# Up projection of an encoder layer: 21 instead of 14 of 64 row pairs by seven products, the transposes of a group together, and an order for VectorE where the stage begins

## The chip, the core and the metric

The kernel runs on one core of a Trainium2 chip. The metric is the device time of one execution in microseconds (us); the time of a kernel is the median over its runs. PE is TensorE (matrix products), DVE is VectorE, ACT is ScalarE, POOL is GpSimd, SP is the engine whose queue issues most of the loads. L649 is line 649 of the kernel.

## What is computed

One layer of an encoder for 256 tokens of 2048 channels: a projection, two kinds of attention, gates, an output projection, and an MLP with squared ReLU. The change lies in the up projection, the first half of the MLP (line 2 below), and a little of it in what stands just ahead.

```python
x = x + rms_norm(y, norm_mix_post)            # y: output projection, 256 x 2048
h = rms_norm(x, norm_mlp_pre)
u = square(relu(h @ w_up))                    # w_up: 2048 x 8192, float32, 64 MB
x = x + rms_norm(u @ w_down, norm_mlp_post)
```

## The kernel before, in words

Products are made in float32 accuracy from halves: a number is split into a high half (a cast to fp32r on ACT, tiles `...h`) and the rest (a subtraction on DVE, tiles `...l`), and each product is three matmuls: high x high, high x low, low x high. The activations are the stationary side (`h2T`, transposed by PE through an identity matrix), the weights the moving side, 512 columns at a time.

**Groups and pairs.** The up projection runs over 8 groups of 1024 columns (`for g in range(DFF // 1024)`); names `u_3h` and so on leave out the group. In a group, `wide_group` runs over 8 pairs of 128-row slices of `w_up` (pair i is 256 rows x 1024 columns, 1 MB, one load by SP, L606). The result of a group stands in PSUM banks 1, 2, 3 and 7 (2 token halves x 2 column halves).

**Eight products.** A pair with eight products (flag 0) casts all of `raw` to `hi` on ACT (L609, 128x2048), takes the rest on DVE (L610), and makes 4 bank pieces x 2 slices x 3 = 24 matmuls.

**Seven products.** A pair with seven (flag 1) is Winograd's form of Strassen's scheme for a 2 x 2 block product: `pair_weights` casts three of the four blocks (L613, 128x1536) and takes their rest (L617), makes four sums of blocks on DVE (L614, L615, L616, tiles `t`), casts these in two pieces (L626, `eh`) and takes their rest (L627, `el`). `Products.seven` then makes 7 x 3 = 21 matmuls: products 2, 1, 0 from the blocks, and 4, 6, 5, 3 from the sums, in banks 0 to 6. The stationary side needs sums too (`h2s`), made once, in group 0, by `sums_of`. At the last pair with seven, `combine` brings banks 0, 4, 5 and 6 together on ACT and DVE (L676 to L680), and each piece then has its plain bank added (`u_piece`, L1022).

**Buffers.** `raw`, `hi` and `lo` have three buffers each (pool `wp`), so a pair's load waits until an earlier pair's `raw` is read for the last time, and its cast until PE has made the last matmul on an earlier pair's `hi` and `lo`. The tiles `eh` and `el` have five buffers (pool `mid`). The sums `t` and most other tiles come from 27 pages of 4 KB in each partition. PSUM has four banks for 1, 2, 3 and 7, and four that banks 0, 4, 5, 6 share with all transposes.

**What comes between.** While a group runs, the previous group's result is turned and split: `u_sets` transposes 512 columns (8 small matmuls `uT`, L1009), squares them on ACT (L1012), makes sums (`sm`, L952 to L955) for every other set, splits them (`ah` on ACT, `al` on DVE, L967, L968) and writes them to DRAM (POOL's queue, L971). There are two sets to a group, one asked for at pair n = 1 and one at n = 2.

**Order.** The kernel is written tile by tile, and a scheduler with a clock of its own sets the order on each engine: the next instruction of an engine is the first in program order that it takes to be ready then. On the chip each engine keeps that order and waits where an operand is late. Matmuls into one PSUM bank keep program order. `tc.issue_after(x)` holds an instruction back behind x in that order.

**Where the stage begins.** The output projection's last group (`agroup`, L230 to L232) makes the rows of token half t = 0, then t = 1. As soon as half 0 is done, its post norm runs on DVE and POOL (`ry_m`, L86; `ry`, L89), the residual is added (L869), and `between` puts the first transposes (L876) among the last matmuls; ACT and DVE split these into `h2T` (L885, L886). Group 0 has eight products throughout; of its first three pairs t = 0 is made first, then the first residual part of t = 1 (`turn`), then t = 1. `first_up(n)` puts the other parts at n = 2 to 4.

Of the kernel before, what the change touches and what calls it, by code (L numbers as in the profile page):

```python
# [11 lines left out]
F32 = mybir.dt.float32  # L12
F32R = mybir.dt.float32r
AF = mybir.ActivationFunctionType
ALU = mybir.AluOpType
# [8 lines left out]
EPS = 1e-6  # L24
# [14 lines left out]
def encoder_layer(ctx: ExitStack, tc: tile.TileContext, a, out):  # L39
    nc = tc.nc  # L40
# [41 lines left out]
    def inv_rms(ss, n, name, r=None):  # L82

        w = ss.shape[1]
        ms_ = small(w, f"{name}_m")
        nc.vector.tensor_scalar(ms_, ss, 1.0 / n, EPS, op0=ALU.mult, op1=ALU.add)  # L86
        if r is None:
            r = small(w, f"{name}_r")
        nc.gpsimd.tensor_tensor(r, ms_, expo[:, :w], op=ALU.pow)  # L89
        return r  # L90


    last_load = [None]

    def load(src, k0, nk, c0, cw, name):

# [502 lines left out]
    def wtile(tag, name):  # L599
        return wp.tile([P, 4, 512], F32R, tag=tag, name=name)  # L600

    def pair_weights(view, name, seven, low=None):


        raw = wp.tile([P, 4, 512], F32, tag="raw", name=f"{name}r")
        last_load[0] = nc.sync.dma_start(raw.rearrange("p (h b) c -> p h (b c)", h=2), view).ins  # L606
        h1, l1 = wtile("hi", f"{name}h"), wtile("lo", f"{name}l")
        if not seven:
            nc.scalar.copy(h1, raw)  # L609
            nc.vector.tensor_sub(l1, raw, h1.bitcast(F32))  # L610
            return h1, l1
        t = [page([P, 2, 512], F32, f"{name}t{i}") for i in range(2)]
        nc.scalar.copy(h1[:, 1:4], raw[:, 1:4])  # L613
        nc.vector.tensor_add(t[0], raw[:, 1:3], raw[:, 0:1].to_broadcast([P, 2, 512]))  # L614
        nc.vector.tensor_add(t[1][:, 0], t[0][:, 0], raw[:, 2])  # L615
        nc.vector.tensor_add(t[1][:, 1], t[1][:, 0], raw[:, 3])  # L616
        nc.vector.tensor_sub(l1[:, 1:4], raw[:, 1:4], h1[:, 1:4].bitcast(F32))  # L617
        h2, l2 = [], []
        for i in range(2):
            for part, n in ((h2, "eh"), (l2, "el")):  # L620
                shape, n = [P, 2, 512], f"{name}{n}{i}"
                if low and part is l2:
                    part.append(low(shape, F32R, n))
                else:
                    part.append(mid.tile(shape, F32R, tag="e", name=n))
            nc.scalar.copy(h2[i], t[i])  # L626
            nc.vector.tensor_sub(l2[i], t[i], h2[i].bitcast(F32))  # L627
        return h1, l1, h2, l2
# [3 lines left out]
    class Products:  # L632
# [22 lines left out]
        def seven(self, stat, w, last):  # L655


            r, t = w[:2], list(zip(*w[2:]))
            self.add(0, stat(0), r, 1, last)
            self.add(2, stat(6), r, 2)  # L660
            self.add(1, stat(1), r, 3)
            self.add(4, stat(3), t[0], 0, last)
            self.add(6, stat(4), t[0], 1, last)
            self.add(5, stat(5), t[1], 0, last)
            self.add(3, stat(2), t[1], 1)
# [16 lines left out]
    def wide_group(name, kinds, view, stat7, stat8, mm_banks, z, piece, each=None, turn=None):  # L682

        any7 = any(s for _, s in kinds)
        pr = Products(name, mm_banks)
        for n, (i, seven) in enumerate(kinds):
            if each:
                each(n)  # L690
            w = pair_weights(view(i), f"{name}_{i}", seven)
# [58 lines left out]
    ALL8 = [(i, 0) for i in range(8)]  # L750
# [22 lines left out]
    for h in range(2):  # L773
        gate = []
        for br, gc in (("a", GA), ("b", GB)):
# [89 lines left out]
    def residual_parts(t, c, after=None):  # L865
        cs = slice((c % 2) * 512, (c % 2 + 1) * 512)
        xt = x2[t * 2 + c // 2][:, cs]
        with tc.issue_after(after) if after else nullcontext():
            nc.vector.scalar_tensor_tensor(  # L869
                xt, yw[t * 2 + c // 2][:, cs], ry[:, t : t + 1], xt, op0=ALU.mult, op1=ALU.add  # L870
            )
        for h in range(2):
            pt = bank(f"h2T_t{t}{c}{h}")
            for i in range(2):
                kk = h * 2 + i
                last = nc.tensor.transpose(  # L876
                    pt[:, i * P : (i + 1) * P], xt[:, kk * P : (kk + 1) * P], ident
                )
            for i in range(2):
                k = c * 4 + h * 2 + i  # L880
                d = hT2[k // 2][:, k % 2]
                src = pt[:, i * P : (i + 1) * P]
                hi = d[:, t * P : (t + 1) * P]
                g = g_mlp[:, k : k + 1]
                act = nc.scalar.activation(hi, src, AF.Copy, scale=g)  # L885
                vec = nc.vector.scalar_tensor_tensor(  # L886
                    d[:, T + t * P : T + (t + 1) * P],
                    src,
                    g,
                    hi.bitcast(F32),  # L890
                    op0=ALU.mult,
                    op1=ALU.subtract,
                )
        return last.ins, act.ins, vec.ins

    def between(i):
        return residual_parts(0, i - 5)[0] if i in (5, 6) else None

    def mlp_squares(t):
        for c in range(4):  # L900
# [25 lines left out]
    def first_up(n):  # L926
        for t, c in {2: [(1, 1), (0, 2)], 3: [(1, 2), (0, 3)], 4: [(1, 3)]}.get(n, ()):
            residual_parts(t, c)
        if n == 5:
            for t in range(2):  # L930
                mlp_squares(t)
                mlp_scale(t)
# [68 lines left out]
    def u_sets(cg, z):  # L1001

        u = page([P, 4, T], F32, f"u{cg}")
        for b in range(2):
            pt = bank(f"uT{cg}{b}")
            for j in range(2):
                for t in range(2):
                    c = (b * 2 + j) * P
                    nc.tensor.transpose(  # L1009
                        pt[:, j * T + t * P : j * T + (t + 1) * P], z[t][:, cg % 2, c : c + P], ident  # L1010
                    )
            nc.scalar.activation(  # L1012
                u[:, b * 2 : b * 2 + 2], pt.rearrange("p (j q) -> p j q", j=2), AF.Square
            )
        got = act_sets(cg, u)
        if NG - 4 <= cg < NG - 2:
            sets[0, cg] = got
# [4 lines left out]
            nc.vector.tensor_add(zt, zt, ps)  # L1022
        nc.scalar.activation(zt, zt if summed else ps, AF.Relu, scale=r2[:, t : t + 1])

    UPS = [(0, 0), (1, 0), (2, 0), (3, 1), (4, 0), (5, 1), (6, 0), (7, 0)]
    uz = None
    for g in range(DFF // 1024):
        z = [page([P, 2, 512], F32, f"u{g}{t}") for t in range(2)]

        def up_each(n, g=g, uz=uz):  # L1030
            if not g:
                first_up(n)
                if n == 7:
                    for i in (3, 5):
                        f = page([P, 2, T], F32, f"h2f{i}")
                        for k in range(2):
                            d = hT2[i][:, k].bitcast(F32)
                            nc.vector.tensor_add(f[:, k], d[:, :T], d[:, T:])
                        h2sum[i] = sums_of(f[:, 0], f[:, 1], f"h2s{i}")
            elif n in (1, 2):  # L1040
                u_sets(g * 2 - 3 + n, uz)

        wide_group(
            f"u{g}",
            UPS if g else ALL8,
            lambda i, c=g * 1024: a["w_up"][i * T : (i + 1) * T, c : c + 1024].rearrange(
                "(k p) c -> p k c", p=P
            ),
            h2stat7,
            h2stat8,  # L1050
            (1, 2, 3, 7),
            z,
            partial(u_piece, z=z),
            each=up_each,
            turn=None if g else partial(residual_parts, 1, 0),
        )
        uz = z

# [140 lines left out]
```

## Time and profile before

| | |
|---|---|
| median of 3 runs | 1370.4 us (1367.77 to 1371.29) |
| profiled execution | 1367.94 us, of which the span is 1366.2 us |
| granted PE clock | 0.997 of full speed |
| PE busy | 1340.7 us, 98% of the span |
| DVE busy | 1034.7 us, 76% |
| ACT busy | 717.8 us, 53% |
| up projection, groups 1 to 7 | about 44 us each (752.28 to 796.29 is one) |

Instructions are told with start, duration, engine, line, and the idle time of their engine just before them in brackets, with what ended it. A row with x3 holds three of a kind. Starts are us from the span's start.

### The profile page before, as it was taken

The page shows a single profiled execution, that of the slowest core. Times are in us where ns is not written, and L with a number is a line of the kernel's source. Part 1 is how long each engine was busy: PE and PEld are TensorE (multiplying, and loading weights), DVE is VectorE, ACT ScalarE, POOL GpSimd, SP SyncE. Part 2 cuts the span into 40 slices and gives each one's busy share as a digit, 9 for nine tenths or more (in the row PEclk, how much of TensorE's full clock was granted, in tenths as well). Part 3 has the DMA queues.
Part 4 walks back from the last instruction along what each step waited for, and adds up shares of the span by engine and source line. Part 5 has one row for each costly group of instructions (what it writes and reads, how often), then busy time and mean ns, then how long its engine had stood idle before and what let it go on. Part 6 is the DMA issues. An engine that isn't in the chain of part 4 may idle for free.

```text
span 1366.2 us, 16268 instructions
## 1 busy us (share of the span) xinstructions
PE 1340.7 (98%) x6347; PEld 1119.4 (82%) x6347; DVE 1034.7 (76%) x1181; ACT 717.8 (53%) x843; POOL 33.9 (2%) x67
## 2 busy tenths in 40 slices
PE   7999999999999999999999999999999999999996
PEld 6888888888888888888788888888887788888885
DVE  6878866667857886654768887888788888798886
ACT  7455455555644464344465655666555555454542
POOL 0000000000000000000000000000000000000000
PEclk9999999999999999999999999999999999999998
DMA  8675645564556655676367766786697999698891
GB/s 306 201 227 168 202 161 175 166 206 154 185 185 213 218 185 185 204 264 205 134 207 260 259 244 243 258 287 231 249 336 282 386 355 373 239 385 346 340 352 74
DMA packets 115245, 329.57 MB, mean 241 GB/s; under 512 B 17120, under 2 KB 18400, under 8 KB 115168
## 3 DMA queue, kind: packets, MB, share of 16 engines
q1 hardware_dynamic: 96784, 264.03, 56.1%
q10 hardware_dynamic: 12240, 40.91, 7.7%
q0 software_dynamic: 6144, 23.60, 4.3%
q8 instruction: 50, 0.82, 0.2%
q14 instruction: 27, 0.22, 0.0%
HBM read 302.81 MB, written 27.51 MB: 242 GB/s over the span
## 4 chain that ended last, share of the span: by engine, by line
PE 96%; DVE 1%; DMA 1%; issue 0%; ACT 0%; ACTq 0%; SPq 0%; DVEq 0%; POOLq 0%; POOL 0%
PE u L649 25%; PE p L649 23%; PE ga L649 6%; PE gb L649 6%; PE ba L649 3%; PE bb L649 3%; PE qa_p L192 2%; PE ka_p L192 2%; PE qn_p L192 2%; PE kn_p L192 2%; PE y_p L230 2%; PE y_p L231 2%; PE y_p L232 2%; PE qa_p L193 1%; PE qn_p L193 1%; PE kn_p L193 1%
## 5 line engine op out<-in xcount | busy, mean ns | idle before, releaser
L117 DVE TENSOR_TENSOR y_l<-y_w,y_h 128x1024 fp32r<-128x1024 f32 x32 | 37.9, 1222 | 30.9 <-ACT y_h L116 30.9
L116 ACT CAST y_h<-y_w 128x1024 fp32r<-128x1024 f32 x32 | 32.0, 1047 | 40.9 <-PE y_p L232 32.6
L230 PE MATMUL y_p<-y_h,mh 128*128 128x512 f32 x128 | 50.1, 391 | 0.0
L231 PE MATMUL y_p<-y_l,mh 128*128 128x512 f32 x128 | 49.9, 390 | 0.0
L232 PE MATMUL y_p<-y_h,ml 128*128 128x512 f32 x128 | 49.8, 390 | 0.0
L192 PE MATMUL qa_p<-hT,qa_h 128*128 128x512 f32 x128 | 47.1, 413 | 1.2 <-DVE hT L275 1.2
L649 PE MATMUL u<-u_0h,h2T 128*128 128x512 f32 x128 | 44.6, 392 | 2.3 <-DVE ry_m L86 1.1
L192 PE MATMUL qn_p<-hT,qn_h 128*128 128x512 f32 x128 | 45.9, 400 | 0.0
L192 PE MATMUL kn_p<-hT,kn_h 128*128 128x512 f32 x128 | 45.4, 398 | 0.0
L192 PE MATMUL ka_p<-hT,ka_h 128*128 128x512 f32 x128 | 45.0, 398 | 0.0
L649 PE MATMUL u<-u_1h,h2T 128*128 128x512 f32 x128 | 44.6, 396 | 0.0
L649 PE MATMUL u<-u_4h,h2T 128*128 128x512 f32 x128 | 42.1, 390 | 0.0
L649 PE MATMUL u<-u_2h,h2T 128*128 128x512 f32 x128 | 41.8, 397 | 0.0
L649 PE MATMUL u<-u_6h,h2T 128*128 128x512 f32 x128 | 41.8, 389 | 0.0
L649 PE MATMUL u<-u_7h,h2T 128*128 128x512 f32 x128 | 41.0, 389 | 0.0
L193 PE MATMUL qn_p<-hT,qn_l 128*128 128x256 f32 x128 | 35.9, 281 | 0.0
L193 PE MATMUL kn_p<-hT,kn_l 128*128 128x256 f32 x128 | 35.7, 280 | 0.0
L193 PE MATMUL qa_p<-hT,qa_l 128*128 128x256 f32 x128 | 35.2, 285 | 0.0
L193 PE MATMUL ka_p<-hT,ka_l 128*128 128x256 f32 x128 | 35.2, 280 | 0.0
L609 ACT CAST u_1h<-u_1r 128x2048 fp32r<-128x2048 f32 x8 | 15.3, 1913 | 36.1 <-PE u L649 32.6
L649 PEld LDWEIGHTS u<-u_0h,h2T 128*128 128x128 f32 x128 | 23.9, 188 | 8.4 <-DVE ry_m L86 1.6
L192 PEld LDWEIGHTS qa_p<-hT,qa_h 128*128 128x128 f32 x128 | 24.6, 194 | 6.7 <-DVE hT L275 1.6
(1386 smaller groups left out, 4346.8 us busy)
## 6 DMA issues: line engine op xcount, KB each, us to landing
y_w<-in_w_out SPq DMA_DIRECT2D x16, 1024.0 KB, 5.3
bh<-keeph ACTq DMA_DIRECT2D x30, 512.0 KB, 9.2
bl<-keepl ACTq DMA_DIRECT2D x30, 512.0 KB, 11.1
keeph<-ah POOLq DMA_DIRECT2D x18, 512.0 KB, 3.4
keepl<-al POOLq DMA_DIRECT2D x18, 512.0 KB, 7.2
ka_w<-in_w_in SPq DMA_DIRECT2D x8, 1024.0 KB, 5.7
va_w<-in_w_in SPq DMA_DIRECT2D x8, 1024.0 KB, 5.0
qn_w<-in_w_in SPq DMA_DIRECT2D x8, 1024.0 KB, 5.1
```

The source lines that it names most:

```text
L116: nc.scalar.copy(hi[part], raw[part])
L117: nc.vector.tensor_sub(lo[part], raw[part], hi[part].bitcast(F32))
L192: nc.tensor.matmul(ps[b], hi[:, k % 4, cs], mv, start=(k == 0), stop=False)
L193: nc.tensor.matmul(ps[b][:, :T], lo[:, k % 4, cs], mv[:, :T], start=False, stop=(k == nk - 1))
L230: nc.tensor.matmul(ps[t], sh, hi[:, k % 4], start=(k == 0), stop=False)
L231: nc.tensor.matmul(ps[t], sh, lo[:, k % 4], start=False, stop=False)
L232: nc.tensor.matmul(ps[t], sl, hi[:, k % 4], start=False, stop=(k == nk - 1))
L609: nc.scalar.copy(h1, raw)
L649: ins = nc.tensor.matmul(self.ps[i], st, mv[:, blk], start=i not in self.begun, stop=last and n == 2).ins
```

## The change

Groups 1 to 7 take the list `MIXED`, with seven products for pairs 0, 3 and 6 in the order 1, 0, 2, 3, 4, 6, 5, 7, instead of `UPS`, with seven for pairs 3 and 5 in the order 0 to 7. Stationary sums are made for pairs 0, 3 and 6 instead of 3 and 5. Both sets of `u_sets` are asked for at n = 1. In `Products.seven`, which the gates and the down projection use too, product 0 comes after 2 and 1. At the stage's beginning the subtraction of pair 1 (`u_1l`) is held behind the last split of the first two parts, and that of pair 2 behind the first step of the second post norm (`scaled[0]`). `turn_rows` does what `partial(residual_parts, 1, 0)` did.

```diff
         if not seven:
             nc.scalar.copy(h1, raw)
-            nc.vector.tensor_sub(l1, raw, h1.bitcast(F32))
+            with tc.issue_after(after) if after else nullcontext():
+                nc.vector.tensor_sub(l1, raw, h1.bitcast(F32))
             return h1, l1
...
             r, t = w[:2], list(zip(*w[2:]))
-            self.add(0, stat(0), r, 1, last)
             self.add(2, stat(6), r, 2)
             self.add(1, stat(1), r, 3)
+            self.add(0, stat(0), r, 1, last)
...
     def between(i):
-        return residual_parts(0, i - 5)[0] if i in (5, 6) else None
+        if i in (5, 6):
+            last, act, vec = residual_parts(0, i - 5)
+            tail.append((act, vec))
+            return last
...
     def first_up(n):
...
+        if n == 1:
+            return tail[1][1]
+        if n == 2:
+            return scaled[0]
...
-    UPS = [(0, 0), (1, 0), (2, 0), (3, 1), (4, 0), (5, 1), (6, 0), (7, 0)]
     # MIXED = [(1, 0), (0, 1), (2, 0), (3, 1), (4, 0), (6, 1), (5, 0), (7, 0)]
...
-                    for i in (3, 5):
+                    for i in (0, 3, 6):
...
-            elif n in (1, 2):
-                u_sets(g * 2 - 3 + n, uz)
+            elif n == 1:
+                for q in (2, 1):
+                    u_sets(g * 2 - q, uz)
...
-            UPS if g else ALL8,
+            MIXED if g else ALL8,
```

What this does to the order, at three places. In the names, `u_6546`, `u_6553`, `u_6560` and `u_6567` (before: 6515, 6522, 6529, 6536) are banks 1, 2, 3 and 7 of group 3, `u_6656` (6679) is bank 0, `u_6660` (6689) bank 4, `u_6664` (6693) bank 6.

PE in group 3, up to the first matmuls of pair 4, before:

```order
L649 MATMUL u_6522<-u_3h,h2s_5779 128x512
L649 MATMUL u_6522<-u_3l,h2s_5779 128x512
L649 MATMUL u_6522<-u_3h,h2s_5779 128x512
L649 MATMUL u_6515<-u_3h,h2T_4850 128x512
L649 MATMUL u_6515<-u_3l,h2T_4850 128x512
L649 MATMUL u_6515<-u_3h,h2T_4850 128x512
L649 MATMUL u_6515<-u_4h,h2T_4851 128x512
L649 MATMUL u_6522<-u_4h,h2T_4851 128x512
L649 MATMUL u_6536<-u_4h,h2T_4851 128x512
L649 MATMUL u_6515<-u_4l,h2T_4851 128x512
```

PE at the same place now; the first row is the last matmul on `u_0h`:

```order
L653 MATMUL u_6656<-u_0h,h2T_4847 128x512
L653 MATMUL u_6656<-u_3h,h2T_4850 128x512
L653 MATMUL u_6553<-u_3l,h2s_5790 128x512
L653 MATMUL u_6553<-u_3h,h2s_5790 128x512
L653 MATMUL u_6546<-u_3l,h2T_4850 128x512
L653 MATMUL u_6546<-u_3h,h2T_4850 128x512
L653 MATMUL u_6656<-u_3l,h2T_4850 128x512
L653 MATMUL u_6656<-u_3h,h2T_4850 128x512
L653 MATMUL u_6546<-u_4h,h2T_4851 128x512
L653 MATMUL u_6553<-u_4h,h2T_4851 128x512
L653 MATMUL u_6567<-u_4h,h2T_4851 128x512
L653 MATMUL u_6546<-u_4l,h2T_4851 128x512
```

Pair 4 stood behind 81 matmuls of the group (24 each of pairs 0, 1 and 2, and 9 of pair 3) and stands behind 60 now (24 of pair 1, 9 of pair 0, 18 of pair 2, 9 of pair 3); six of pair 2, those into bank 3, have moved behind pair 0's sums, which go into bank 3 first.

PE in group 3, up to the first matmuls of pair 6, before (they follow the 18 of pair 4):

```order
L649 MATMUL u_6679<-u_5h,h2T_4852 128x512
L649 MATMUL u_6522<-u_5h,h2s_5790 128x512
L649 MATMUL u_6515<-u_5h,h2T_4852 128x512
L649 MATMUL u_6689<-u_3eh_6671,h2s_5779 128x512
L649 MATMUL u_6693<-u_3eh_6671,h2s_5779 128x512
L649 MATMUL u_6679<-u_5l,h2T_4852 128x512
L649 MATMUL u_6679<-u_5h,h2T_4852 128x512
L649 MATMUL u_6522<-u_5l,h2s_5790 128x512
L649 MATMUL u_6522<-u_5h,h2s_5790 128x512
L649 MATMUL u_6515<-u_5l,h2T_4852 128x512
L649 MATMUL u_6515<-u_5h,h2T_4852 128x512
L649 MATMUL u_6515<-u_6h,h2T_4853 128x512
```

PE at the same place now; the first two rows are the last of the 18 matmuls of pair 4:

```order
L653 MATMUL u_6567<-u_4l,h2T_4851 128x512
L653 MATMUL u_6567<-u_4h,h2T_4851 128x512
L653 MATMUL u_6660<-u_0eh_6642,h2s_5779 128x512
L653 MATMUL u_6664<-u_0eh_6642,h2s_5779 128x512
L653 MATMUL u_6553<-u_6h,h2s_5801 128x512
L653 MATMUL u_6546<-u_6h,h2T_4853 128x512
L653 MATMUL u_6656<-u_6h,h2T_4853 128x512
```

Between the 18 matmuls of pair 4 and the first of pair 6 stood 11 others, and two stand now.

DVE where the stage begins, from the residual on, before:

```order
L869 SCALAR_TENSOR_TENSOR x_0_4829<-yw_4837,ry,x_0_4829 128x512 x2
L869 SCALAR_TENSOR_TENSOR x_1_4830<-yw_4838,ry,x_1_4830 128x512 x2
L610 TENSOR_TENSOR u_1l<-u_1r,u_1h 128x2048
L886 SCALAR_TENSOR_TENSOR h2T_4847<-h2T_t_5393,g_mlp,h2T_4847 128x128
L886 SCALAR_TENSOR_TENSOR h2T_4848<-h2T_t_5400,g_mlp,h2T_4848 128x128
L886 SCALAR_TENSOR_TENSOR h2T_4849<-h2T_t_5411,g_mlp,h2T_4849 128x128
L886 SCALAR_TENSOR_TENSOR h2T_4850<-h2T_t_5418,g_mlp,h2T_4850 128x128
L918 TENSOR_TENSOR yw_4840<-y_p_5264,gpost_4826 128x512
L862 TENSOR_REDUCE sy_5434<-ssy_4842 128x1
L610 TENSOR_TENSOR u_2l<-u_2r,u_2h 128x2048
L886 SCALAR_TENSOR_TENSOR h2T_4847<-h2T_t_5393,g_mlp,h2T_4847 128x128
L86 TENSOR_SCALAR ry_m<-sy_5434 128x1
```

DVE at the same place now (`u_2l` is the next row after these):

```order
L889 SCALAR_TENSOR_TENSOR h2T_4847<-h2T_t_5393,g_mlp,h2T_4847 128x128
L889 SCALAR_TENSOR_TENSOR h2T_4848<-h2T_t_5400,g_mlp,h2T_4848 128x128
L889 SCALAR_TENSOR_TENSOR h2T_4849<-h2T_t_5411,g_mlp,h2T_4849 128x128
L889 SCALAR_TENSOR_TENSOR h2T_4850<-h2T_t_5418,g_mlp,h2T_4850 128x128
L889 SCALAR_TENSOR_TENSOR h2T_4847<-h2T_t_5393,g_mlp,h2T_4847 128x128
L889 SCALAR_TENSOR_TENSOR h2T_4848<-h2T_t_5400,g_mlp,h2T_4848 128x128
L889 SCALAR_TENSOR_TENSOR h2T_4849<-h2T_t_5411,g_mlp,h2T_4849 128x128
L929 TENSOR_TENSOR yw_4840<-y_p_5264,gpost_4826 128x512
L865 TENSOR_REDUCE sy_5434<-ssy_4842 128x1
L889 SCALAR_TENSOR_TENSOR h2T_4850<-h2T_t_5418,g_mlp,h2T_4850 128x128
L614 TENSOR_TENSOR u_1l<-u_1r,u_1h 128x2048
L86 TENSOR_SCALAR ry_m<-sy_5434 128x1
```

The subtractions `u_1l` and `u_2l` have moved behind the splits `h2T` of the first half, and the first step of the second norm (`ry_m`) from behind `u_2l` to ahead of it. ACT has moved its casts likewise: three of the four splits that stood behind `u_2h` stand ahead of the square `jy`, the fourth just behind it.

More of the change, by code (lines that the diff above doesn't have):

```diff
@@ L85, in inv_rms @@
         ms_ = small(w, f"{name}_m")
-        nc.vector.tensor_scalar(ms_, ss, 1.0 / n, EPS, op0=ALU.mult, op1=ALU.add)
+        scaled[0] = nc.vector.tensor_scalar(
+            ms_, ss, 1.0 / n, EPS, op0=ALU.mult, op1=ALU.add
+        ).ins
         if r is None:
@@ L93, in encoder_layer @@
     last_load = [None]
+    scaled = [None]
     def load(src, k0, nk, c0, cw, name):
@@ L600, in wtile, with pair_weights @@
         return wp.tile([P, 4, 512], F32R, tag=tag, name=name)
-    def pair_weights(view, name, seven, low=None):
+    def pair_weights(view, name, seven, low=None, after=None):
         raw = wp.tile([P, 4, 512], F32, tag="raw", name=f"{name}r")
@@ L688, in wide_group @@
         for n, (i, seven) in enumerate(kinds):
-            if each:
-                each(n)
-            w = pair_weights(view(i), f"{name}_{i}", seven)
+            after = each(n) if each else None
+            w = pair_weights(view(i), f"{name}_{i}", seven, after=after)
             if seven:
@@ L894, in residual_parts, with turn_rows @@
         return last.ins, act.ins, vec.ins
+    tail = []
     def between(i):
-        return residual_parts(0, i - 5)[0] if i in (5, 6) else None
+        if i in (5, 6):
+            last, act, vec = residual_parts(0, i - 5)
+            tail.append((act, vec))
+            return last
+    def turn_rows():
+        residual_parts(1, 0)
     def mlp_squares(t):
@@ L1031, in up_each @@
             if not g:
-                first_up(n)
+                after = first_up(n)
                 if n == 7:
-                    for i in (3, 5):
+                    for i in (0, 3, 6):
                         f = page([P, 2, T], F32, f"h2f{i}")
@@ L1039, in up_each @@
                         h2sum[i] = sums_of(f[:, 0], f[:, 1], f"h2s{i}")
-            elif n in (1, 2):
-                u_sets(g * 2 - 3 + n, uz)
+                return after
+            elif n == 1:
+                for q in (2, 1):
+                    u_sets(g * 2 - q, uz)
         wide_group(
             f"u{g}",
-            UPS if g else ALL8,
+            MIXED if g else ALL8,
             lambda i, c=g * 1024: a["w_up"][i * T : (i + 1) * T, c : c + 1024].rearrange(
@@ L1054, in encoder_layer @@
             each=up_each,
-            turn=None if g else partial(residual_parts, 1, 0),
+            turn=None if g else turn_rows,
         )
```

## The prediction

> **What bounds the kernel now.** I read the page first, then each engine's time in the stretches around the change, then rows in order of time in one group of the up projection and where the stage begins.
>
> ```profile
> span 1366.2 us, 16268 instructions
> PE 1340.7 (98%) x6347; PEld 1119.4 (82%) x6347; DVE 1034.7 (76%) x1181; ACT 717.8 (53%) x843; POOL 33.9 (2%) x67
> 320.00:480.00 160.00, 160.00 (x723) 133.03 (x722) 119.59 (x118) 78.26 (x66) 0.00 (x0) 1.00 0.57 193
> 752.28:796.29 44.01, 44.01 (x204) 36.52 (x202) 35.69 (x35) 25.84 (x26) 3.23 (x6) 1.00 0.74 258
> 1095.00:1116.00 21.00, 21.00 (x94) 17.40 (x93) 19.14 (x16) 10.60 (x8) 0.00 (x0) 1.00 0.91 354
> ```
>
> In the stretches the columns are PE, PEld, DVE, ACT and POOL busy. PE never pauses in the gates (third row), in a group of the up projection (fourth) or in the down projection (fifth). DVE does 35.7 of 44.0 us of the group.
>
> What a matmul costs is its distance to the next, not its length, since they overlap:
>
> ```profile
> 766.82 0.61 PE L649 MATMUL u<-u_2h,h2T 128*128 128x512 f32 x2
> ...
> 770.00 0.39 PE L649 MATMUL u<-u_2l,h2T 128*128 128x512 f32 x1
> ```
>
> Fourteen matmuls begin from the first row until the second: 3.18 / 14 = 0.227 us each, against a length of 0.39. A group has 6 x 24 + 2 x 21 = 186, so 42.2 us; the other 1.8 of the 44.0 are 16 transposes, 0.11 each.
>
> The Trainium skill (Perfetto Trace Analysis, Identifying the Most-Contended Engine) calls matmul busy time a bad measure, and names weight loads as the good one. By PEld's 82% PE would have room, the matmuls saved would gain nothing, and the sum below would be 4.8 us longer. The trace does not bear that out: 36.52 / 44.01 is 83% where no gap is left.
>
> **How far ahead of PE the halves are.** This decides the forecast. Rows of the next group, which begins at 796.29:
>
> ```profile
> 805.83 0.42 DVE L953 TENSOR_TENSOR sm<-u 128x256 f32<-128x256 f32 x1
> 802.65 1.47 ACT L613 CAST u_3h<-u_3r 128x1536 fp32r<-128x1536 f32 x1 [1.75 <-issue]
> 808.30 1.05 ACT L967 CAST ah<-sm 128x1024 fp32r<-128x1024 f32 x1 [1.29 <-DVE sm L955]
> 809.25 1.91 ACT L609 CAST u_4h<-u_4r 128x2048 fp32r<-128x2048 f32 x1
> 811.19 2.29 DVE L610 TENSOR_TENSOR u_4l<-u_4r,u_4h 128x2048 fp32r<-128x2048 f32 x1 [0.58 <-ACT u_4h L609]
> 813.51 0.37 SPq L606 DMA_DIRECT2D u_6r<-in_w_up  x1
> 817.23 0.39 PE L649 MATMUL u<-u_4l,h2T 128*128 128x512 f32 x1
> 820.71 1.92 ACT L609 CAST u_6h<-u_6r 128x2048 fp32r<-128x2048 f32 x1 [3.57 <-DMA u_6r<-in_w_up]
> 823.12 0.84 PE L649 MATMUL u<-u_6h,h2T 128*128 128x512 f32 x3
> DMA to landing us min/median/max: 5.0/6.3/7.4
> ```
>
> `u_4l` ends at 813.48 and PE asks for it at 817.23, 3.7 us later. Its end frees the buffer for pair 6's load (0.03 us later), which takes 5.0 to 7.4 us (last row, all eight of `u_6r`); ACT waits 3.57 us for it, and its cast ends at 822.63, 0.5 us before PE wants it. So the chain u_4l, load, cast is hidden by 0.5 us.
>
> **The change part by part.**
>
> Matmuls: seven groups lose one pair of 24 for one of 21: 7 x 3 x 0.227 = 4.8 us. A group without a wait would take 183 x 0.227 + 1.8 = 43.4.
>
> DVE and ACT, per group:
>
> ```profile
> L610 DVE TENSOR_TENSOR u_6l<-u_6r,u_6h 128x2048 fp32r<-128x2048 f32 x7 | 16.0, 2288 | 1.7 <-ACT u_6h L609 1.7
> L627 DVE TENSOR_TENSOR u_3el<-u_3t,u_3eh 128x1024 fp32r<-128x1024 f32 x14 | 17.1, 1220 | 0.0
> L617 DVE TENSOR_TENSOR u_3l<-u_3r,u_3h 128x1536 fp32r<-128x1536 f32 x6 | 10.6, 1758 | 10.7 <-ACT u_3h L613 10.7
> L614 DVE TENSOR_TENSOR u_3t<-u_3r 128x1024 f32<-128x1024 f32 x7 | 8.5, 1219 | 0.0
> L616 DVE TENSOR_TENSOR u_3t<-u_3t,u_3r 128x512 f32<-128x512 f32 x7 | 4.8, 686 | 0.0
> ```
>
> Another pair with seven costs DVE 1.76 + 1.22 + 2 x 0.69 + 2 x 1.22 - 2.29 = 4.5 us: 40.2 of 43.4, 93%. The down projection runs at 19.14 / 21.00 = 91% without a gap on PE, so load alone costs nothing. ACT gains 1.47 + 2 x 1.05 - 1.91 = 1.7 us on 25.8: hidden by its 18 idle us.
>
> PE's new order costs most. Walk a group from its first matmul (0), in the order shown, with the durations above. Pair 4 now stands behind 60 matmuls and 16 transposes: 60 x 0.227 + 1.8 = 15.4. Its `hi` buffer is pair 0's, whose last matmul is the eighth before it: begun at 52 x 0.227 + 1.8 = 13.55, ended 0.39 later, at 13.95. But ACT comes later. `u_3h` takes pair 1's buffer, whose last matmul follows 31 others and 4 transposes: begun at 7.5, ended at 7.9; the cast ends at 9.4 and `u_3l`, 1.76, at 11.1. Then come the set's sums and splits, as from 805.83 to 808.30 (2.45): 13.5. `ah<-sm` delays the next cast by 0.95, and `u_4h` lasts from 14.4 to 16.35, `u_4l` to 18.65. Three matmuls need only `u_4h`: 1.0 us late, 16.4 to 17.05. The fourth needs `u_4l`: 18.7, another 1.65. So 2.65 us are lost at pair 4, where 3.7 were to spare.
>
> After it come 15 matmuls of pair 4 and two of pair 0's sums, up to 22.55. Then PE asks for `u_6h`. Its load leaves at 18.7 and lands 6.3 later, at 25.0; the cast, 1.47, ends at 26.55: PE waits 4.05 us. Together 6.7 a group. Queued behind `u_6h` on ACT are pair 0's and 3's `eh` casts, and behind PE's wait everything else of the group; walking on, `u_3eh`, `u_5h`, `u_5l`, `u_6eh` and `u_7l` come 0.6 us or more ahead, so I add no further wait.
>
> The Trainium skill (DMA: Bandwidth & Descriptors, Anatomy of one DMA) fits a transfer as 2.0 us and its bytes at 436 GB/s, 4.4 us for this load. By it the wait would be 1.9 us less, and the sum 13 us less. The row's minimum of 5.0 is above it already; the trace decides, and neither this rule nor the one on weight loads is given a chance.
>
> Bounds for the waits: least, if ACT takes `u_4h` as soon as PE is done with pair 0 (13.95, 0.45 earlier) and the load lands in 5.0: 4.95. Most, at 7.4: 7.8. I take 6.7, by the median, in six groups. In group 1 four more matmuls of pair 0's sums stand ahead of pair 6, and 0.9 of the wait is filled: 5.8. Sum: 6 x 6.7 + 5.8 - 4.8 = +41 us; bounds 7 x 4.95 - 4.8 = +30 and 7 x 7.8 - 4.8 = +50.
>
> Where the stage begins:
>
> ```profile
> 657.10 1.13 ACT L885 ACTIVATE h2T<-h2T_t,g_mlp 128x128 fp32r<-128x128 f32 x4
> 657.54 2.29 DVE L610 TENSOR_TENSOR u_1l<-u_1r,u_1h 128x2048 fp32r<-128x2048 f32 x1
> 658.76 0.39 PE L649 MATMUL u<-u_0h,h2T 128*128 128x512 f32 x1
> 658.96 0.60 ACT L916 ACTIVATE jy<-y_p 128x512 f32<-128x512 f32 x1 [0.73 <-PE y_p L232]
> 659.74 1.12 DVE L886 SCALAR_TENSOR_TENSOR h2T<-h2T_t,g_mlp,h2T 128x128 fp32r<-128x128 f32 x4
> 659.86 0.37 SPq L606 DMA_DIRECT2D u_4r<-in_w_up  x1
> 660.14 0.73 PE L649 MATMUL u<-u_0h,h2T 128*128 128x512 f32 x2 [0.31 <-DVE h2T L886]
> 661.75 0.50 PE L649 MATMUL u<-u_0h,h2T 128*128 128x512 f32 x1 [0.88 <-ACT h2T L885]
> 664.08 0.72 PE L649 MATMUL u<-u_0h,h2T 128*128 128x512 f32 x2 [1.12 <-DVE ry_m L86]
> 664.77 2.74 DVE L869 SCALAR_TENSOR_TENSOR x<-yw,ry,x 128x512 f32<-128x512 f32 x4
> 671.01 0.39 PE L649 MATMUL u<-u_0h,h2T 128*128 128x512 f32 x1
> ```
>
> From 658.76 to 671.01 PE does 36 matmuls and 8 transposes, 9.05 us of work in 12.25. Now DVE begins the splits at 657.55 (0.28 each), ACT makes seven of eight before `jy`, and pair 0 runs through from 658.76 to 661.5. `yw` follows `jy` (659.75), and `sy` and the last split end at 660.75; `u_1l` lasts until 663.05. PE, after two matmuls with `u_1h`, wants it at 661.95: 1.1 us late. `u_2l` ends at 665.3, ahead of PE's 665.8. The last row's matmul moves to 668.95: 2.1 us gained. The residual of t = 1 begins behind `u_2l`, at 665.3 instead of 664.77; its first two parts end at 666.65, and PE reaches their transposes at 668.05. On SP's queue the load of pair 4 leaves when `u_1l` ends, 3.2 us later than at 659.86; pair 4's cast comes after PE is done with pair 1, past 670, so this is covered. Bounds: nothing, if a wait moves in front of them, and 3.2, all that was lost.
>
> Third set of stationary sums:
>
> ```profile
> 692.26 0.75 DVE L1038 TENSOR_TENSOR h2f<-h2T 128x256 f32<-128x256 f32 x2
> 693.19 0.28 DVE L719 TENSOR_TENSOR h2s3s<-h2f 128x128 f32<-128x128 f32 x1
> 698.49 2.29 DVE L610 TENSOR_TENSOR u_7l<-u_7r,u_7h 128x2048 fp32r<-128x2048 f32 x1 [1.38 <-ACT u_7h L609]
> 700.96 0.68 DVE L724 TENSOR_TENSOR h2s<-h2s3s,h2s 128x512 fp32r<-128x512 f32 x1
> 703.70 0.39 PE L649 MATMUL u<-u_7l,h2T 128*128 128x512 f32 x1
> 979.61 0.49 PE L649 MATMUL u<-u_1l,h2T 128*128 128x512 f32 x1
> ```
>
> The third set is 0.75 + 4 x 0.28 + 0.68 = 2.55 us of DVE. The 1.4 idle and the lead of 2.9 (700.78 to 703.70) hide them; without that cover it would cost 1.1. Transposes together: the same 16, in two blocks instead of three; the first matmul behind a block lasts 0.49 (last row) instead of 0.39, so a block less gives 0.1 at most, 0.7 in all; I take 0. The POOL queue's writes keep their count, and SP's loads go in the pairs' new order: 0. Product 0 as third in the gates and the down projection: the same matmuls where PE has no gap; 0, within 0.5.
>
> The sum is 1367.9 - 2.1 + 41 = 1407 against the profiled execution, which is 2.5 below the median of the runs (1370.4); against that, 1409. I say 1408, with 1398 to 1419 from the bounds.
>
> **Rivals.** What a measurement of this kernel can tell is about 0.3%, 4 us.
>
> Faster: PE's lead holds. If `u_6h` came by 20 us in the group, both waits would be gone, and 4.8 + 2.1 come off: 1363.5. Its load would have to leave by 12.2, while `u_4h` cannot begin before 13.95; for it speaks only that no group of before waits. Below about 1.0 us of wait a group it decides. 0.09; another 0.03 for no change.
>
> Only pair 4 waits, since pair 6's load finds another buffer: 7 x 2.65 - 4.8 - 2.1 = +11.7, 1382. The row at 813.51, right behind `u_4l`, speaks against it. 0.08.
>
> More waits: `u_6t` needs pages that the writes of the sets give back. One of these takes up to 17:
>
> ```profile
> DMA to landing us min/median/max: 2.8/7.5/17.0
> ```
>
> (`keepl`; its median is harmless.) Two us more a group would give 1422. 0.05.
>
> **How the numbers follow.** The forecast has 0.75. The range takes in the rival at 1382: 1380 to 1419, which leaves out 0.17. Faster 0.09, the same 0.03, slower 0.88.
>
> **What would show it.** In groups 1 to 7 PE waits twice: for `u_4h` and `u_4l`, 2.65 us together, and for `u_6h`, about 4, and ACT ahead of `u_6h` waits for the load. A group lasts about 50 us, and has 183 matmuls. Where the stage begins, PE waits once, for `u_1l`, about 1.1. I am wrong if PE shows no wait at pair 6, which would mean that loads or buffers come earlier than I walked them.

## The result, and the profile after

The changed kernel takes 1420.24 us (median of 4 runs, 1419.44 to 1422.19), the kernel before 1369.37 beside it. The ratio is 1.0378, with a 95% interval of 1.036 to 1.0396: 51 us slower. The profiled execution took 1422.19 us, with a span of 1420.4. Ratios here and below leave out one execution that took twice as long as its like, 2747.55 us (of the kernel with late sets alone).

The page of the changed kernel; PE was busy 98% of the span before:

```profile
span 1420.4 us, 16307 instructions
PE 1355.4 (95%) x6326; PEld 1123.0 (79%) x6326; DVE 1066.4 (75%) x1223; ACT 728.5 (51%) x858; POOL 36.0 (3%) x67
PE 82%; DVE 6%; DMA 4%; ACT 4%; issue 3%; ACTq 0%; SPq 0%; DVEq 0%; POOLq 0%
```

The third row is the chain that ended last. It no longer runs on PE alone. Groups 1 to 7 of the up projection as one stretch, the kernel before first, then the changed one (PE, PEld, DVE, ACT and POOL busy, granted clock, DMA share, GB/s):

```profile
708.24:1016.64 308.40, 308.40 (x1416) 255.61 (x1415) 247.55 (x236) 179.89 (x173) 22.68 (x42) 1.00 0.74 260
```
```profile
704.77:1070.98 366.21, 324.56 (x1395) 259.90 (x1393) 278.75 (x272) 190.07 (x188) 22.80 (x42) 0.96 0.64 221
```

The whole loss is here: 366.21 instead of 308.40, 57.8 us in seven groups. They begin 3.5 us earlier: 2.1 come from the stage's beginning, and 1.5 from the first 33 us of the kernel, where nothing was changed (0.8 of them are a shorter wait for the input). 349.4 us follow them (349.6 before), so the span grows by 54.2. The granted clock fell to 0.96. What PE waited for, in total, times, and the longest:

```profile
PE u L653 <- ACT u_6h L617: 23.6, 7, 4.4
PE u L653 <- DVE u_4l L614: 9.5, 7, 1.4
PE u L653 <- ACT u_4h L612: 5.9, 7, 1.0
PE u L653 <- DVE u_0el L631: 1.7, 1, 1.7
PE u L653 <- ACT u_0eh L630: 0.8, 1, 0.8
```

These are 41.5 us; the kernel before had none in these groups. In the group that begins at 859.16, the rows at pairs 4 and 6:

```profile
873.81 1.90 ACT L612 CAST u_4h<-u_4r 128x2048 fp32r<-128x2048 f32 x1
875.76 0.96 PE L653 MATMUL u<-u_4h,h2T 128*128 128x512 f32 x3 [0.99 <-ACT u_4h L612]
878.06 0.37 SPq L609 DMA_DIRECT2D u_6r<-in_w_up  x1
878.08 0.50 PE L653 MATMUL u<-u_4l,h2T 128*128 128x512 f32 x1 [1.36 <-DVE u_4l L614]
884.99 1.47 ACT L617 CAST u_6h<-u_6r 128x1536 fp32r<-128x1536 f32 x1 [3.60 <-DMA u_6r<-in_w_up]
886.52 0.80 PE L653 MATMUL u<-u_6h,h2s 128*128 128x512 f32 x1 [4.25 <-ACT u_6h L617]
888.39 0.63 PE L653 MATMUL u<-u_0eh,h2s 128*128 128x512 f32 x1
888.82 0.63 PE L653 MATMUL u<-u_0el,h2s 128*128 128x512 f32 x1
...
892.64 0.39 PE L653 MATMUL u<-u_6h,h2T 128*128 128x512 f32 x1
892.87 0.39 PE L653 MATMUL u<-u_6l,h2T 128*128 128x512 f32 x1
```

Pair 6's load leaves when `u_4l` ends, ACT waits 3.60 us for it, and PE 4.25 for the cast. Then comes what no step of the prediction had: after the wait, matmuls start 0.43 us apart and last 0.63, and only from 892.64 on 0.23 and 0.39 again. The same place in windows of 3.41 us, with one of group 1 ahead:

```profile
728.69:732.10 3.41, 1.69 (x6) 1.12 (x7) 2.72 (x4) 2.02 (x2) 0.00 (x0) 1.00 0.90 280
732.10:735.51 3.41, 3.41 (x10) 2.16 (x9) 3.41 (x4) 2.40 (x3) 0.00 (x0) 0.51 0.60 178
...
875.46:878.87 3.41, 1.75 (x6) 1.16 (x7) 3.13 (x2) 2.27 (x4) 1.07 (x2) 1.00 0.71 290
878.87:882.28 3.41, 3.40 (x15) 2.44 (x13) 3.38 (x5) 1.06 (x1) 0.53 (x1) 1.00 0.90 213
882.28:885.70 3.42, 0.00 (x0) 0.00 (x0) 2.88 (x4) 0.71 (x1) 0.00 (x0) 1.00 1.03 411
885.70:889.11 3.41, 2.59 (x6) 2.11 (x7) 3.17 (x4) 2.66 (x3) 0.00 (x0) 0.51 0.76 294
889.11:892.52 3.41, 3.41 (x9) 2.64 (x9) 3.22 (x4) 1.05 (x1) 0.00 (x0) 0.50 0.77 238
```

The eighth number (behind POOL's) is the granted clock. PE stood still from 882.28 to 885.70, and the next window was granted half the clock; that window held six matmuls, and the one behind it was at half again. There are nine such windows in groups 1 to 7. Each follows a window in which PE was busy for some 1.7 us or less of 3.41, or the window at half clock with six matmuls; after the one at 875.46, with 1.75 us, the full clock stayed. The windows' edges are known to about 0.1 us, and the other runs don't sharpen the limit: in the kernel with two pairs, below, the full clock stayed after a window with 1.69 us (886.65), and in the one with three in a row half the clock followed one with 2.08 (732.30). So the limit lies near half a window, between some 1.7 and 2.1 us, and busy time alone doesn't settle it there.

Where the stage begins, PE runs through pair 0, waits 0.84 us at `u_1l`, and reaches the second half 10.15 us after the first (12.25 before):

```profile
657.23 0.39 PE L653 MATMUL u<-u_0h,h2T 128*128 128x512 f32 x1
661.42 0.50 PE L653 MATMUL u<-u_1l,h2T 128*128 128x512 f32 x1 [0.84 <-DVE ry_m L86]
667.38 0.50 PE L653 MATMUL u<-u_0h,h2T 128*128 128x512 f32 x1
```

### The profile page after: what moved, and what is told of

Its sections match the earlier page's. It is cut to its first block, busy times and chain, and to the rows that moved or that the text cites. A ratio compares the mean times of both kernels' runs of the same rounds, so it can differ in the third digit from the quotient of the medians.

```text
span 1420.4 us, 16307 instructions
## 1 busy us (share of the span) xinstructions
PE 1355.4 (95%) x6326; PEld 1123.0 (79%) x6326; DVE 1066.4 (75%) x1223; ACT 728.5 (51%) x858; POOL 36.0 (3%) x67
## 4 chain that ended last, share of the span: by engine, by line
PE 82%; DVE 6%; DMA 4%; ACT 4%; issue 3%; ACTq 0%; SPq 0%; DVEq 0%; POOLq 0%
PE p L653 19%; PE u L653 17%; PE ga L653 6%; PE gb L653 6%; PE ba L653 3%; PE bb L653 3%; DMA u_6r<-in_w_up 3%; PE qa_p L195 2%; PE ka_p L195 2%; PE qn_p L195 2%; PE kn_p L195 2%; PE y_p L234 2%; PE y_p L233 2%; PE y_p L235 2%; DVE u_4l L614 1%
## 5 line engine op out<-in xcount | busy, mean ns | idle before, releaser
L653 PE MATMUL u<-u_4h,h2T 128*128 128x512 f32 x128 | 45.5, 417 | 5.9 <-ACT u_4h L612 5.9
L653 PE MATMUL u<-u_5h,h2T 128*128 128x512 f32 x128 | 41.9, 389 | 0.0
L653 PE MATMUL u<-u_4l,h2T 128*128 128x512 f32 x64 | 27.2, 425 | 9.5 <-DVE u_4l L614 9.5
L621 DVE TENSOR_TENSOR u_3l<-u_3r,u_3h 128x1536 fp32r<-128x1536 f32 x7 | 12.3, 1758 | 31.5 <-ACT u_3h L617 31.5
L196 PE MATMUL qn_p<-hT,qn_l 128*128 128x256 f32 x128 | 35.9, 281 | 0.0
L653 PEld LDWEIGHTS u<-u_4h,h2T 128*128 128x128 f32 x128 | 24.8, 198 | 13.7 <-ACT u_4h L612 8.9
L617 ACT CAST u_0h<-u_0r 128x1536 fp32r<-128x1536 f32 x7 | 10.4, 1486 | 48.5 <-PE u L653 48.3
```

The costliest lines, as they stand in the source:

```text
L196: nc.tensor.matmul(ps[b][:, :T], lo[:, k % 4, cs], mv[:, :T], start=False, stop=(k == nk - 1))
L653: ins = nc.tensor.matmul(self.ps[i], st, mv[:, blk], start=i not in self.begun, stop=last and n == 2).ins
```

## The experiments

Each was compared with the kernel before on the same chip, which took 1367.9 to 1368.9 us there; intervals are of the ratio to it.

**The old list alone.** Is the list the whole loss?

```diff
+    UPS = [(0, 0), (1, 0), (2, 0), (3, 1), (4, 0), (5, 1), (6, 0), (7, 0)]
...
-                    for i in (0, 3, 6):
+                    for i in (3, 5):
...
-            elif n == 1:
-                for q in (2, 1):
-                    u_sets(g * 2 - q, uz)
+            elif n in (1, 2):
+                u_sets(g * 2 - (2 if n == 1 else 1), uz)
...
-            MIXED if g else ALL8,
+            UPS if g else ALL8,
```

> The changed kernel with the old list again (seven products for pairs 3 and 5, two sets of sums, one set of transposes at n = 1 and one at n = 2). What stays of the change is the order where the stage begins and product 0 as third. Theory (the list is the whole loss): no wait in groups 1 to 7, groups of 44.0 us, and the 2.1 us gained where the stage begins are kept: 1365.5 to 1368, that is 1.5 to 4 below the kernel before. Rival (one of the other edits holds part of the 51 us): 1372 or more.

1365.97 us against 1368.28, ratio 0.9981 (0.9972 to 0.9989). Groups 1 to 7, as one stretch:

```profile
707.02:1015.37 308.35, 308.35 (x1415) 255.66 (x1414) 247.67 (x236) 180.00 (x173) 22.75 (x42) 1.00 0.74 260
```

They are as long as before, and 2.3 us remain of the stage's beginning. So list and sets hold the whole loss, and the order where the stage begins is worth what the walk gave it.

**Filling PE's wait.** Does the slow stretch follow PE's idle time, or what runs beside it?

```diff
+            if self.name[0] == "u" and 5 not in self.ps:
+                self.ps[5] = bank(f"{self.name}5", False)
+                for _ in range(18):
+                    nc.tensor.matmul(
+                        self.ps[5], stat(3)[0], t[0][0][:, 0], start=True, stop=True
+                    )
             self.add(5, stat(5), t[1], 0, last)
```

> The changed kernel with 18 extra matmuls a group on operands that are ready, put into the PSUM bank of product 5 ahead of that bank's own first matmul, which overwrites them. They stand where PE waits for u_6h. Theory (clock): PE falls to half rate for 3.41 us after a window of 3.41 us in which it was busy for less than half. 18 x 0.227 = 4.1 us fill the wait of 4.3 us, so eight or nine of the nine stretches at half rate go, 1.6 us each: 13 to 14 us less. In groups 1, 3 and 7 the waits were 1.29, 2.55 and 2.79, and the fill is longer by 2.8, 1.5 and 1.3: 5.6 more. Together 1410 to 1415, with 126 matmuls more. Rival (PE is slowed there by what runs beside it, the casts and loads): the stretches stay and the extra matmuls cost their 5.6 or more: 1425 or above.

1415.45 us, ratio 1.0348 (1.0333 to 1.0362), 4.8 less than the changed kernel's median with 126 matmuls more. The intervals of the two ratios just touch, but the stretch of groups 1 to 7 (last row here) shows the gain too, 359.56 us instead of 366.21. The fill and what follows it in one group:

```profile
782.63 4.24 PE L671 MATMUL u<-u_0eh,h2s 128*128 128x512 f32 x18
786.71 0.39 PE L653 MATMUL u<-u_6h,h2s 128*128 128x512 f32 x1
786.94 0.62 PE L653 MATMUL u<-u_6h,h2T 128*128 128x512 f32 x2
...
706.97:1066.53 359.56, 341.69 (x1520) 277.52 (x1519) 278.65 (x272) 190.93 (x188) 22.78 (x42) 0.99 0.65 226
```

Pair 6 runs at full speed right behind the fill, while the same casts and loads go on. Three windows at half clock are left of nine in these groups, each behind the two waits at pair 4 where these fall into one window (and one came in the down projection). That is fewer than I expected to go (I had not counted that those two waits can do it alone), and 0.5 us above the range. The rival falls: PE's own idle time lowers the clock.

**A fourth buffer for loads.** Is the chain `u_4l`, load, cast what holds PE at pair 6? The tag `raw` gets `bufs=4`, and the pool `pages` 25 instead of 27.

> The changed kernel with four buffers for the loaded weights instead of three, and 25 pages instead of 27 to make room. The load of pair 6 then takes pair 2's buffer and leaves when u_2l ends, some 12 us earlier. Theory (u_4l, load, cast is the chain that holds PE at pair 6): ACT no longer waits for this load, the 23.6 us of waits for u_6h go but for what the cast behind u_4h leaves, about 2 us a group, and most of the stretches at half rate with them; the waits at pair 4 (15.4 us together) stay: 1420 less 23.6, plus 14, less 10: about 1400, between 1388 and 1410, the upper half if the two pages are missed elsewhere. Rival (PE would wait at pair 6 anyway, for ACT or DVE): 1415 or more.

1400.58 us, ratio 1.0232 (1.0218 to 1.0246). The longest waits:

```profile
PE u L653 <- ACT u_6h L617: 9.5, 7, 1.4
PE u L653 <- ACT u_4h L612: 5.9, 7, 1.0
PE u L653 <- ACT u_0eh L630: 5.2, 5, 1.4
PE u L653 <- DVE u_0el L631: 3.2, 3, 1.8
```

ACT casts `u_6r` right behind `u_4h`, without a wait for the load, and the 23.6 us become 9.5. These 9.5 are no longer behind pair 4: PE now takes its first matmul on `u_6h` right behind the first three on `u_4h`, ahead of `u_4l`, so the wait there, 1.37 us a group, has changed its name and not its length. Three windows at half clock remain. The chain is shown; the waits at pair 4 stay, and pair 0's sums, still late on DVE, are next.

**Two pairs with seven, in the same places.** Place or number?

```diff
+    UPS = [(1, 0), (0, 1), (2, 0), (3, 1), (4, 0), (6, 0), (5, 0), (7, 0)]
...
-                    for i in (0, 3, 6):
+                    for i in (0, 3):
...
-            MIXED if g else ALL8,
+            UPS if g else ALL8,
```

> The changed kernel with seven products for pairs 0 and 3 alone, in the same places (second and fourth); pair 6 gets eight again. DVE has 4.5 us a group less to do, so its load is the one of the kernel before. Theory (the place decides: pair 4 stands behind too few matmuls and its buffer is pair 0's): the waits at pairs 4 and 6 stay as they are, and a group has three matmuls more: 1415 to 1428. Rival (the number decides, through DVE at 93%): no waits, 1363 to 1372.

1428.27 us, ratio 1.0437 (1.0421 to 1.0453): slower than with three, and 0.3 above the range.

```profile
PE u L653 <- ACT u_6h L612: 12.3, 7, 1.8
PE u L653 <- DVE u_0el L631: 10.3, 6, 1.7
PE u L653 <- DVE u_4l L614: 9.5, 7, 1.4
...
707.52:1075.35 367.83, 331.33 (x1416) 261.40 (x1414) 251.39 (x237) 182.21 (x175) 22.79 (x42) 0.96 0.62 221
```

DVE has 251 us of work here, 4 more than before the change, and the stretch is 1.6 us longer than with three. So neither the number of pairs with seven nor the load of DVE is what costs. My expectation that the waits stay "as they are" was wrong in their shares: `u_6h` has 12.3 instead of 23.6, and pair 0's `el` 10.3 instead of 1.7.

**Without the sets' work.** What stands ahead of pair 4's cast and pair 0's sums? This kernel leaves out work that the result needs; its time only shows what that work holds up.

```diff
+        if 2 <= cg < NG - 4:
+            for i in range(2 if seven_of(cg) else 1):
+                for n in "hl":
+                    kept[cg, i, n] = kept[cg % 2, i, n]
+            return
         got = act_sets(cg, u)
```

> The changed kernel without the sums, splits and writes of the sets in groups 2 to 6 (the transposes and squares stay; the down projection reads the sets of group 1 in their place). DVE and ACT lose some 6.8 and 3.0 us a group. Theory (it is the sets' work, which stands ahead, that holds up the casts and sums): groups 2 to 6 run without a wait, 43.4 us each, instead of 52.3: 1420 less 45, 1370 to 1382. Rival (list and buffers alone: u_4h can't begin before PE is done with pair 0): by the walk u_4h then begins at 13.95 and u_4l ends at 18.2, pair 6's load lands at 24.5, so about 6 of the 6.7 us a group and most stretches at half rate stay: 1405 or more.

1375.56 us, ratio 1.0055 (1.0041 to 1.0069). Groups 2 to 6:

```profile
757.14:974.32 217.18, 217.18 (x996) 179.79 (x995) 179.71 (x157) 124.91 (x117) 0.00 (x0) 1.00 0.56 194
```

217.18 / 5 = 43.44 us a group, the 43.4 of the walk without a wait. List, buffers and loads are those of the changed kernel, so it is the sets' work that stands in the way. Whether by its amount or by its place this run can't tell, since the writes are gone with it; the next three keep all of it. (DVE has 35.9 us a group here and ACT 25.0, against 39.8 and 27.2: 3.9 and 2.2 less, not the 6.8 and 3.0 I had put there.) My rival was the walk with that work taken out and everything else left in place; it fell, because the order changes with it: the first matmuls on pair 0's sums move ahead of pair 4.

**Pair 0's sums first.** In the changed kernel `u_0t`, the first of pair 0's sums of blocks, comes behind both sets on DVE, although `u_0l` reads the same `raw` at 858.77 already, and DVE idled ahead of `u_3l`:

```profile
868.65 1.76 DVE L621 TENSOR_TENSOR u_3l<-u_3r,u_3h 128x1536 fp32r<-128x1536 f32 x1 [4.73 <-ACT u_3h L617]
877.95 1.22 DVE L983 TENSOR_TENSOR al<-u,ah 128x1024 fp32r<-128x1024 f32 x1
879.08 1.22 DVE L618 TENSOR_TENSOR u_0t<-u_0r 128x1024 f32<-128x1024 f32 x1
```

In `wide_group`, for groups 1 to 7, the weights of a pair are now written ahead of the sets:

```diff
-            after = each(n) if each else None
+            late = each and name[0] == "u" and name != "u0"
+            after = each(n) if each and not late else None
             w = pair_weights(view(i), f"{name}_{i}", seven, after=after)
+            if late:
+                each(n)
```

> The changed kernel with pair 0's load, cast and sums of blocks written ahead of the two sets (u_sets) in groups 1 to 7; list and places stay. Theory (the sets stand ahead of u_0t on DVE, so pair 0's products from the sums come behind pair 4 on PE): now these 12 matmuls and pair 2's last six stand ahead of pair 4, 4.1 us, which is more than the 2.65 us that pair 4 was late, and the waits at pair 4 (15.4 us) go; a wait at pair 6 or 5 may stay where the sets' work is pushed: 1395 to 1410. Rival (DVE has too much to do in any order, 93%): 1415 to 1425.

1394.28 us, ratio 1.0191 (1.0174 to 1.0209), 0.7 below the range. The waits at pair 4 are gone; PE now waits elsewhere, mostly

```profile
PE u L653 <- ACT u_5h L612: 7.9, 7, 2.0
PE u L653 <- DVE u_0l L621: 6.9, 6, 1.3
```

**The sets' work late.** The transposes and squares stay at n = 1 (transposes share PSUM banks with the sums' products); their sums, splits and writes are a function of their own, `u_split` (`act_sets` and what follows it), asked for at n = 5, in group 7 at n = 7:

```diff
-                    u_sets(g * 2 - q, uz)
+                    turned[q] = u_sets(g * 2 - q, uz)
+            if g:
+                for q, at in ((2, (5 if g < 7 else 7)), (1, (5 if g < 7 else 7))):
+                    if n == at:
+                        u_split(g * 2 - q, turned[q])
```

> The changed kernel with the sets' sums, splits and writes asked for at n = 5 (group 7: n = 7) alone; pair 0's load, cast and sums stay behind the transposes in program order. It completes the square: neither edit 1420, sums first alone 1394, both 1358. Theory (the sets' work that stands ahead is the larger part, the place of pair 0's load and cast the smaller): 1370 to 1395, below sums first alone. Rival (either edit alone leaves the same): 1394 or more.

1371.92 us, ratio 1.002 (1.001 to 1.003). This edit is the larger part, but one wait stays, 1.5 us for `u_4l` in each of groups 2 to 6:

```profile
PE u L653 <- DVE u_4l L614: 7.6, 6, 1.5
```

Both edits together:

> The changed kernel with all of its 21 pairs with seven, but pair 0's load, cast and sums written ahead of the sets, and the sets' sums, splits and writes asked for at n = 5 (in group 7 at n = 7) while their transposes and squares stay at n = 1. Theory (the place of the sets' work, not the number of pairs with seven): groups of 43.4 to 44.2 us without half rate, 304 to 309 instead of 366: 1357 to 1364. Rival (with 21 pairs DVE, 93% busy, falls behind once the sets' work lands later in the group): waits of 3 us or more a group, 1380 or more.

1358.05 us, ratio 0.9929 (0.9917 to 0.9942): 9.9 us less than the kernel before, with all 21 pairs with seven. Against the 1420 of the changed kernel, pair 0's sums first take off 26 us, late sets 48, and both 62.

```profile
PE 1334.5 (98%) x6326; PEld 1117.6 (82%) x6326; DVE 1063.1 (78%) x1223; ACT 726.8 (54%) x858; POOL 35.9 (3%) x67
...
706.24:1009.48 303.24, 303.24 (x1395) 252.31 (x1393) 273.80 (x270) 189.52 (x188) 21.40 (x40) 1.00 0.73 256
```

Seven groups take 303.24 us, 43.3 each, without a wait or a window at half clock, although DVE is busy for 90% of them. Rows of the group that begins at 836.17 show why:

```profile
831.12 1.22 DVE L618 TENSOR_TENSOR u_0t<-u_0r 128x1024 f32<-128x1024 f32 x1
838.06 0.68 DVE L620 TENSOR_TENSOR u_0t<-u_0t,u_0r 128x512 f32<-128x512 f32 x1
838.81 0.37 SPq L609 DMA_DIRECT2D u_4r<-in_w_up  x1
839.86 2.28 DVE L614 TENSOR_TENSOR u_2l<-u_2r,u_2h 128x2048 fp32r<-128x2048 f32 x1
842.17 0.37 SPq L609 DMA_DIRECT2D u_6r<-in_w_up  x1
851.59 1.92 ACT L612 CAST u_4h<-u_4r 128x2048 fp32r<-128x2048 f32 x1 [2.02 <-PE u L653]
856.15 0.84 PE L653 MATMUL u<-u_4h,h2T 128*128 128x512 f32 x3
```

Pair 0's sums read its `raw` for the last time at 838.74, so that buffer serves pair 4 at 838.81, and pair 6 takes pair 2's at 842.17, 6.0 us into the group instead of 18.9. With pair 0's products from the sums ahead of it, PE asks for pair 4 at 20.0 us, 2.6 after its cast has ended, where the changed kernel asked 15.5 us into its group.

**The old list with late sets.** How much of this is the third pair with seven? The list, sums and beginning of the first experiment, with all transposes at n = 1 and the rest at n = 7.

> The old list (pairs 3 and 5) with the order where the stage begins and product 0 as third, and the sets' sums, splits and writes asked for at n = 7, all transposes at n = 1. The groups have no wait with the old list anyway, so they stay at 44.0 us. Theory (what the late sets bring, they bring to 21 pairs with seven alone): 1363 to 1367, as with the sets in their old place, and 0 to 5 above the kernel with 21 pairs and late sets. Rival (late sets gain by themselves, at the change to the down projection): 1356 to 1361.

1363.7 us, ratio 0.9968 (0.9955 to 0.998). Its seven groups take 307.98 us, and the kernel with 21 pairs 303.24: 4.74 between them, the 4.8 that the matmuls are worth. The medians lie 5.7 apart. What late sets bring, they bring to the 21 pairs; with the old list the medians 1365.97 and 1363.7 are 2.3 us apart, a sixth of a per cent, and the intervals of the two ratios overlap.

**Three in a row.** The pairs in the order 0 to 7, seven products for 3, 4 and 5, sets as in the change.

> The changed kernel with the pairs in the order 0 to 7 and seven products for pairs 3, 4 and 5, after three pairs with eight; the sets where the change has them (n = 1). PE then has 72 matmuls, 16 us, while the sets' work is done. Theory (PE keeps its lead only where DVE's work is spread like PE's): three pairs with seven in a row ask 3 x 6.8 = 20.4 us of DVE while PE has 63 matmuls, 14.3 us, on them: about 4 to 6 us of waits a group and a stretch at half rate in some: 1390 to 1410. Rival (only the early place of the first pair with seven costs): no wait, 1358 to 1364.

1392.39 us, ratio 1.017 (1.0154 to 1.0185); groups 1 to 7:

```profile
706.77:1035.32 328.55, 315.53 (x1395) 250.24 (x1393) 279.37 (x272) 191.89 (x188) 22.70 (x42) 0.99 0.68 243
```

46.9 us a group instead of the 43.3 of the kernel with both edits, somewhat less lost than I expected: with the sets at n = 1, a lead of three pairs with eight doesn't carry PE through three with seven in a row.

## Why the prediction was wrong in size

**The waits: right in place, and nearly in size.** The walk gave 1.0 us at `u_4h`, 1.65 at `u_4l` and 4.05 at `u_6h`; the trace has 0.99, 1.36 and 4.25. The walk counted lost starts, and the trace counts idle time, behind the modelled end of the matmul ahead. At each of the 23 waits the overlap of 0.16 us (0.39 less 0.227) and 0.11 us of a longer first matmul (0.50) are lost too, 6.2 together, so the waits are, by this estimate, 41.5 + 6.2 = 47.7 against a forecast of 46.0. That the sums agree so well is partly luck: counted so, groups 2, 4, 5 and 6 lost 7.3 to 7.5 us each instead of 6.7, and group 3 lost 5.7, since PE ran at half clock between `u_4l` and `u_6h` there, came later and waited 2.55. The load took 5.1, 6.8 and 8.2 us (least, median, most) instead of 5.0, 6.3 and 7.4. The Trainium skill gives the fit that the prediction works 4.4 us out of (DMA: Bandwidth & Descriptors, Anatomy of one DMA) for transfers on GpSimd's path; this load is issued by SP, and all eight of them took longer. The fourth buffer showed that this load is the chain.

**The matmuls saved: right.** 4.74 us with and without the third pair, where neither waits.

**The step that failed: the clock was left out.** "A group without a wait would take 183 x 0.227 + 1.8" and the sum took every matmul behind a wait at 0.227 us too. Nine windows of 3.41 us ran at half clock, where a matmul costs 0.43: 3.41 x (1 - 0.227 / 0.43) = 1.6 us each, 14.5 together. The seven groups lost 57.8 against 41 forecast; of the 16.8 between, 14.5 are the clock by this account, and 1.7 the waits. That put the result 51 us above the kernel before instead of 39, just past the upper bound, which had the longest load in it and no clock. The fill shows that the clock follows PE's idle time. The view that has it is the granted clock in windows behind a wait, and the kernel before has no wait in groups 1 to 7. Its start could have been a warning: behind waits of 4.29, 2.13 and 1.20 us, a matmul of 512 columns and one of 256 take 0.64 us together (10.62 to 11.26), and 0.35 later (15.64 to 15.99).

The Trainium skill (TensorE: Matmul & The Clock Gate, Part 1: The HAM clock gate) describes this: a window of 3413 ns that runs free, and half the clock after an idle one. The trace agrees on the window: 732.10 and 885.70 lie 45 x 3.413 us apart. Its advice (HAM oscillation) is to avoid idle gaps above some 3.4 us. Here that would be too mild: in group 1 no wait was longer than 1.69 us, and two waits that left PE 1.69 us of one window busy were enough. The prediction left the rule out, though it forecast a wait of 4.05 us.

**The work of DVE and ACT: right as load, incomplete as cause.** At 90% of the stretch DVE delays nothing where the sets' work comes late. The walk had the sets' sums and splits in it, ahead of `u_4h`, and met the trace there: the cast began 14.65 us into the group at 859.16, 14.4 in the walk. But it took that order as given, and where the prediction asked what could remove the waits it named a buffer ("`u_4h` cannot begin before 13.95"). That bound doesn't bind: with both edits the cast begins at 15.4, and PE asks for it at 20.0. The runs show that what decides is where the sets' work stands: without it, or with it late and pair 0's sums early, the same list runs at 43.3 to 43.4 us a group.

**Where the stage begins: right.** 2.1 us, with one wait of 0.84 where 1.1 was forecast. The third set of sums and product 0 as third cost nothing that shows: from the start of the second half to group 1 it is 37.39 us (37.23 before), and the rest behind the groups 349.4 (349.6). Nor do the transposes together: the old list with all of them at n = 1, and with late sets, has 307.98 us in its groups, and 308.35 with them apart.

**The rivals.** The place of buffers (1382) was the fourth buffer's case, but that left other waits and ended at 1400. "More waits" had the right time, 1422, by a mechanism that didn't occur: `u_6t` waited for the load, not for pages.

What stays open: why pair 0's `el` takes over the waits where pair 6 has eight, and what settles the clock after a window that is about half busy. Neither was tried.

## What to carry to other kernels

When a pair of products with fewer matmuls moves forward, walk the order of every engine, not only PE's: what stands ahead of the new producers in program order decides whether PE's lead holds. Moving work that is not urgent (here the sums, splits and writes for a later stage) behind the producers turned a loss of 51 us into a gain of 10. Price a wait with its aftermath: in these runs, where PE was busy for less than about half of a 3.41-us window, the next one cost 1.6 us more.

## What the hardware showed that I had not expected

Two short waits are enough for half clock, if they fall into one window: at 824.26 PE was busy for 1.26 us, after waits of 0.99 and 1.36, and ran at half clock until about 831.1. A window at half clock with little work in it was followed by another (885.70, six matmuls; in the kernel with two pairs also 838.86, six). And extra work made the kernel faster: 126 matmuls more took 4.8 us off.
